# Earlier weight sums in the up projection, VectorE adds in the merges, and a first weight cast in two pieces: a two-layer hybrid decoder on one core

## The chip, the core and the metric

The kernel runs on one core of a Trainium2 chip. The core has five engines that work side by side, each with an instruction queue of its own: TensorE (in the profile PE, with its weight loads as PEld), VectorE (DVE), ScalarE (ACT), GpSimd (POOL) and SyncE (SP), which here only issues DMAs. GpSimd and ScalarE issue DMAs too. An engine takes its instructions in order; when the first one waits on a semaphore, what is behind it waits too. Matrix products are accumulated in PSUM, and everything else lives in SBUF.

The metric is the device time of one execution in microseconds (us), and the time of a kernel is the median over several executions.

## The reference

`reference()` is a trunk of `DEPTH` = 2 layers over `SEQ` = 512 tokens of width `D_MODEL` = 1024, all in float32. Cut to what matters:

```python
for l in range(DEPTH):
    h = rmsnorm(x, norm1_g[l])
    p = h @ w_in[l]
    p_rw, p_ret, p_sg, gate_logits = jnp.split(p, in_cuts, axis=-1)
    branches = jnp.stack([y_rw, y_ret, y_sg], axis=2)   # three token mixers
    proj = jnp.einsum('bsgc,gcd->bsgd', branches, w_branch[l])
    gates = jax.nn.sigmoid(gate_logits.reshape(B, S, N_BRANCH, D_MODEL))
    x = x + jnp.sum(gates * proj, axis=2) @ w_out[l]
    x = x + conv_ffn(rmsnorm(x, norm2_g[l]), ffn_w_up[l], ffn_conv_w[l], ffn_conv_b[l], ffn_w_down[l])
return rmsnorm(x, final_g)
```

`conv_ffn` multiplies by `ffn_w_up` (1024 x 5632), applies a causal convolution of width 3 along the tokens, multiplies silu(gate) by the value half, and multiplies by `ffn_w_down` (2816 x 1024).

## The kernel before

**Precision.** TensorE's fast format keeps only part of a float32 number. So each factor is split into a high part (a cast, by ScalarE) and a low part (the number less its high part, by VectorE), and each product is three matmuls: high by low, high by high, low by high (`mm3`, L190; the matmuls are booked under L194). A weight is read in units of 128x512: a load from HBM (`load`, L124, issued by SP into a tile `wr`), a cast (`part`, L175, tiles `wh` or `sh`) and a subtraction (L178, tiles `wl` or `sl`). A unit feeds twelve matmuls. The first pass over the program only notes the units in order; in the second pass this list is the plan by which loads and casts run some units ahead of the products (`unit`, L97; `AHEAD`, L32). The first unit of the plan has `npart` 0.

**The order of work.** The Tile framework orders the instructions of every engine with its own model of their times. `keep_in_program_order` and `kept` (L119) pin the instructions that they are given to the order of the program. In the feed-forward part the loads, casts and subtractions of the weights are kept so, and the weight sums below with them. Tiles come from pools: `acc` has four PSUM buffers, `f`, `u` and `r` hold SBUF tiles of 128x512.

**The start.** `firstK` (L369) multiplies the first units by the first blocks of x. The first weight, the first blocks of x and their norm factors are loaded in turns; a string of steps (L438) gives the order of casts (`w`) and norm products (`z`). A block's high part is made by VectorE for the first block and by ScalarE (L260) for the others, its low part by VectorE (L261). The first unit's matmuls are those of L383, the later ones those of L194.

**The merges.** For each of three branches and eight row blocks, `merge` (L1144) loads a stored gate (`gth<-gd`, L1148, a DMA on GpSimd's queue), multiplies one unit of branch weights by the branch's output into an `acc` tile, and multiplies gate and product on VectorE (L1151). Branch 0 starts the sum `mg[m]`; branch 2 and branch 1 add to it (L1154). For branch 2 (`br` 2, the digit 2 in `SEQ`, L30) GpSimd adds, and for branch 1 VectorE, since only that call passes `add` (L531). After branch 1 the sum is split into its parts (`split`, L182) for the output projection `wout` (L1157).

**The up projection.** `ffn_up` (L1174) computes 44 columns of 128 rows each, a gate column and a value column in turns, numbered `c` from 0. A column takes two units, 24 matmuls. VectorE takes it out of PSUM (L1202, tile `fu`), ScalarE and VectorE do the convolution (L1204 to L1206, tile `cv`), and after each second column come silu and the product (L1213, L1214). Every four columns the results are combined and split for the down projection (`halves`, L1224).

**The weight sums.** The down projection is a Strassen-like scheme that needs sums of blocks of `ffn_w_down`. A set is four raw 128x512 tiles of one block of that weight; from it four sums are made in place. In the up projection `presum` (L283) is called after every column: by the table `PRE` (L27), a set with start `at` has one raw tile loaded (L289, on SP's queue) in each of the columns `at` to `at`+3, and one sum made (L162, on VectorE) and stored to HBM (L304, on GpSimd's queue) in each of the columns `at`+4 to `at`+7. Layer 0 has nine sets, starting every four columns from 4 to 36, so that there is exactly one sum in each of the columns 8 to 43. Layer 1 has six, from 4 to 36, with gaps. The other sets are made elsewhere. The down projection (`down`, L1265, in layer 0; `last`, L1418, in layer 1) reads the sums back as weight units.

Of the kernel before, what the change touches and what calls it, by code (L numbers as in the profile page):

```python
# [13 lines left out]
ADD, SUB, MUL, POW, MAX = ALU.add, ALU.subtract, ALU.mult, ALU.pow, ALU.max  # L14
# [9 lines left out]
FIRST = (12, 4, 0, 8)  # L24
FILL = (36, 2, 1)
KEPT = 6
PRE = {0: {4 + 4 * k: 2 + k for k in range(9)}, 1: {4: 0, 10: 1, 16: 2, 22: 3, 29: 4, 36: 6}}  # L27
RSUM = {(0, 3): (0, 0), (0, 10): (0, 1), (1, 3): (1, 8), (1, 10): (1, 10)}
NOW = ((1, 5), (1, 7), (1, 9))
SEQ = "0 H G G 0 S 0 U U G G 0 S 0 0 S 2 2 Y 0 0 2 1 2 1 2 1 2 1 2 1 2 1 1 1"  # L30
# [23 lines left out]
class Emit:  # L54
# [109 lines left out]
    def part(self, u):  # L164
        raw, n, pool = self.raws.pop(0), u[4], u[5]
        if type(raw) is tuple:
            raw = self.sumnow(raw)

        self.turn = (self.turn + 1) % 5 if pool in ("p", "q") else 4
        if pool is None or self.turn < 3:  # L170
            hi, lo = [self.wp.tile([128, 512], F32R, name=self.nm(t), tag=t, bufs=3) for t in ("wh", "wl")]
        else:
            hi, lo = [{"f": self.f, "r": self.r, "u": self.u, "p": self.u, "q": self.u}[pool](dt=F32R, n=t) for t in ("sh", "sl")]
        with self.tc.high_priority() if pool in (None, "p", "q") else nullcontext():
            self.kept(self.nc.scalar.copy(hi[:, :n], raw[:, :n]))  # L175
            if self.raws and type(self.raws[0]) is tuple:
                self.sumnow(self.raws[0])
            self.kept(self.nc.vector.tensor_tensor(lo[:, :n], raw[:, :n], hi[:, :n], op=SUB))  # L178
        self.parts.append((hi, lo))
        self.npart += 1  # L180
# [102 lines left out]
    def presum(self, l, c):  # L283

        for at, q in PRE[l].items():
            n = c - at
            if 0 <= n < 4:
                self.pre[l, q, n] = t = (self.f if at < 21 else self.u if l or at in (28, 36) else self.r)(n="pre")
                self.kept(self.nc.sync.dma_start(t, self.raw4(l, q, (1, 3, 0, 2)[n])))  # L289
            if 4 <= n < 8:  # L290
                b = [self.pre[l, q, k] for k in (2, 0, 3, 1)]
                p = (7, 5, 6, 4)[n - 4]
                t, i = self.sum4(b, p)
                self.kept(i)
                self.stores.append(((l, q), p, t))
                self.store4(n=1)
# [188 lines left out]
    def mixer(self, l, nst):  # L485
        self.pool = None
        with self.tc.tile_pool(name=f"rw{l}", bufs=1) as rp:
            self.rwp = rp
            self.filler = self.fillers(l)
            st = self.rwkv(l, nst)  # L490
        for _ in self.filler:
            pass
        self.rp = self.tc.tile_pool(name=f"ff{l}", bufs=NFP)
        self.fp = self.rp.__enter__()
        self.gup, self.bs, self.ws = self.f(n="gup"), self.f((128, 4, 128), n="bs"), self.f((128, 4, 128), n="ws")
        with self.tc.high_priority():
            self.nc.sync.dma_start(self.gup, self.a["gup"][l])
        self.nc.sync.dma_start(self.bs.rearrange("p g i -> p (g i)"), self.a["sgb"][l:l + 1, :].to_broadcast([128, 512]))
        self.nc.sync.dma_start(self.ws, self.a["sgw"][l])
        self.pool = "f"  # L500
        sg, out = self.sgu_v(l), self.rwkv_out(l, *st)
        self.nc.vector.tensor_tensor(self.ws, self.ws, self.c("le").unsqueeze(1).to_broadcast([128, 4, 128]), op=MUL)
        self.qk = []
        for c in range(NC):
            self.qk.append(self.f(n="qkT"))
            self.turned(self.qk[c], self.f(n="qkt"), self.ro[c], self.nc.gpsimd)
        self.wsp = self.split(self.ws.rearrange("p g i -> p (g i)"), self.f)
        for step in (sg, sg, out, sg, out, sg, None, out, sg, out, sg):
            next(step) if step else self.sgu_bias()
        yrw, ysg, mg, out, m2 = self.yrw, [], [], [], 0  # L510
        self.pool = "r"
        rest = self.sgu_u(l, range(2, 4))
        rows = iter([((), (0, 1), (0, 1, 2)), ((0, 1), (2, 3)), ((2, 3),)])
        for step in SEQ.split():
            if step == "S":
                self.ret_pair(*next(rows))
            elif step == "G":
                ysg.append(self.sgu_out(len(ysg)))
            elif step == "H":
                self.ret_heads()  # L520
            elif step == "U":
                next(rest), next(rest)
            elif step == "Y":
                yret = self.ret_out()
            elif step == "0":
                mg.append(self.merge(l, 0, len(mg), yrw))
            elif step == "2":
                mg[m2] = self.merge(l, 2, m2, ysg, mg[m2])
                m2 += 1
            else:  # L530
                out.append(self.split(self.merge(l, 1, len(out), yret, mg[len(out)], self.nc.vector), self.f))  # L531
        return out

    def fillers(self, l):
# [606 lines left out]
        return self.split(t2, self.f)  # L1141


    def merge(self, l, br, m, y, sum=None, add=None):  # L1144

        nc = self.nc
        t = self.f(n="gth")
        nc.gpsimd.dma_start(t, self.gd[br, m])  # L1148
        ps = self.acc()
        self.matF(ps, ("wall", l, 58 + br * 4 + m // 2, m % 2 * 512), y)  # L1150
        nc.vector.scalar_tensor_tensor(t, t, 1.0, ps, op0=ADD, op1=MUL)  # L1151
        if sum is None:
            return t
        (add or nc.gpsimd).tensor_tensor(sum, sum, t, op=ADD)  # L1154
        return sum

    def wout(self, l, mg, xd, st):  # L1157
# [566 lines left out]
```

## Time and profile before

| | us |
|---|---|
| median of 3 runs (1688.55, 1686.04, 1684.36) | 1686.04 |
| the profiled execution | 1686.46 |
| its span, from the first to the last instruction | 1684.7 |

| engine | busy us | share of the span |
|---|---|---|
| TensorE, matmuls | 1673.6 | 99% |
| TensorE, weight loads | 1392.5 | 83% |
| VectorE | 1292.1 | 77% |
| ScalarE | 820.3 | 49% |
| GpSimd | 301.4 | 18% |

The granted clock of TensorE is 1.000 over the whole span. In layer 0 the last merges run from about 417 to 465 us, the up projection from about 500 to 733 and the down projection from there; in layer 1 the last merges run from about 1256 to 1304, and the up projection ends at about 1572.

A row of the timeline gives the start, the duration, engine, line and operation, what is written from what is read, the shape and the count, and in brackets how long the engine was idle before it and which instruction ended that. Durations of neighbouring rows overlap a little, because an engine starts the next instruction while the last one still writes; the cost of one in a full queue is the distance of the starts. A row of the waits gives who waited for whom, the total, how many times, and the longest. Matmul ends are modelled and reach past the start of the next matmul.

### The profile page before, as it was taken

Reading aid. Unit: us, or ns where it says so; the run is one execution under the profiler, and the core shown is the slowest. Engines: PE = TensorE matmul, PEld = TensorE weight load, DVE = VectorE, ACT = ScalarE, POOL = GpSimd, SP = SyncE. Lnnn points to the kernel's source line nnn. Section 1 sums busy time; section 2 is a strip of 40 time slices with the busy share of each in tenths; the row PEclk is TensorE's granted clock in tenths of the full one; section 3 lists DMA queues with packets and bytes.
Section 4 is the critical chain, followed back from the end, with each engine's and each line's share of the span. In section 5 each row is a group of like instructions: output and inputs, shape, how many; then the busy total and the mean of one; then the engine's idle time right before and its main releaser. Section 6 shows DMA issues by size and latency. Waiting matters only on the chain.

```text
span 1684.7 us, 29297 instructions
## 1 busy us (share of the span) xinstructions
PE 1673.6 (99%) x10643; PEld 1392.5 (83%) x10643; DVE 1292.1 (77%) x2289; ACT 820.3 (49%) x1436; POOL 301.4 (18%) x450
## 2 busy tenths in 40 slices
PE   9999999999999999999999999999999999999998
PEld 7888877888888888889988887778888888888887
DVE  7887746578668888877868877565785688898897
ACT  6563433554254444456655634335542544444565
POOL 1121013312210111110111210233122012221100
PEclk9999999999999999999999999999999999999999
DMA  5236655533553666678733366655344436664775
GB/s 183 88 109 205 192 185 172 186 125 128 177 188 115 204 202 217 219 233 301 234 114 94 106 195 188 201 164 188 122 143 149 156 131 201 207 209 161 273 243 176
DMA packets 158592, 298.38 MB, mean 177 GB/s; under 512 B 21936, under 2 KB 32944, under 8 KB 158448
## 3 DMA queue, kind: packets, MB, share of 16 engines
q1 hardware_dynamic: 128864, 217.12, 40.2%
q0 software_dynamic: 21232, 64.25, 11.5%
q10 hardware_dynamic: 8352, 15.15, 2.5%
q8 instruction: 83, 1.36, 0.3%
q14 instruction: 61, 0.50, 0.1%
HBM read 236.40 MB, written 60.03 MB: 176 GB/s over the span
## 4 chain that ended last, share of the span: by engine, by line
PE 87%; DVE 5%; issue 3%; DMA 3%; ACT 1%; POOL 1%; SPq 1%; ACTq 0%; DVEq 0%; POOLq 0%
PE acc L194 75%; PE sm L194 5%; PE sm L769 2%; DMA wr<-wall 1%; PE sm L1025 1%; DVE sl L178 1%; PE sm L676 1%; DVE cv L1205 1%; DVE fu L1202 1%; SPq L726 1%; DVE cv L1206 1%; DMA tr<-vT 0%; DVE wl L178 0%; PE sm L1136 0%; ACT cv L1204 0%
## 5 line engine op out<-in xcount | busy, mean ns | idle before, releaser
L194 PE MATMUL acc<-lo,sh 128*128 128x512 f32 (+1 forms) x1144 | 443.0, 387 | 0.4 <-DVE gth L1151 0.4
L194 PE MATMUL acc<-hi,sh 128*128 128x512 f32 (+1 forms) x1144 | 441.8, 386 | 0.0
L194 PE MATMUL acc<-hi,sl 128*128 128x512 f32 (+1 forms) x1144 | 429.3, 386 | 0.5 <-DVE sl L178 0.5
L175 ACT CAST sh<-wr 128x512 fp32r<-128x512 f32 x352 | 212.2, 616 | 213.2 <-DMA wr<-wall 100.5
L175 ACT CAST wh<-wr 128x512 fp32r<-128x512 f32 x278 | 171.4, 620 | 270.8 <-PE acc L194 178.7
L178 DVE TENSOR_TENSOR wl<-wr,wh 128x512 fp32r<-128x512 f32 x278 | 196.2, 708 | 136.7 <-ACT wh L175 130.8
L178 DVE TENSOR_TENSOR sl<-wr,sh 128x512 fp32r<-128x512 f32 x352 | 239.9, 695 | 72.3 <-ACT sh L175 63.5
L194 PEld LDWEIGHTS acc<-lo,sh 128*128 128x128 f32 x1144 | 214.9, 188 | 45.1 <-issue 1.4
L194 PEld LDWEIGHTS acc<-hi,sl 128*128 128x128 f32 x1144 | 214.9, 188 | 44.1 <-DVE sl L178 0.9
L194 PEld LDWEIGHTS acc<-hi,sh 128*128 128x128 f32 x1144 | 214.9, 188 | 42.8
L194 PE MATMUL acc<-lo,wh 128*128 128x512 f32 (+1 forms) x636 | 245.1, 385 | 0.2 <-ACT wh L175 0.2
L194 PE MATMUL acc<-hi,wl 128*128 128x512 f32 (+1 forms) x636 | 243.3, 383 | 0.1
L194 PE MATMUL acc<-hi,wh 128*128 128x512 f32 (+1 forms) x636 | 242.5, 381 | 0.0
L1204 ACT ACTIVATE cv<-fu,pc 128x512 f32<-128x512 f32 x88 | 71.8, 816 | 175.1 <-DVE fu L1202 175.0
L194 PEld LDWEIGHTS acc<-hi,wl 128*128 128x128 f32 x636 | 119.6, 188 | 25.1 <-DVE wl L178 1.4
L194 PEld LDWEIGHTS acc<-lo,wh 128*128 128x128 f32 x636 | 119.6, 188 | 24.3 <-ACT wh L175 1.0
L194 PEld LDWEIGHTS acc<-hi,wh 128*128 128x128 f32 x636 | 119.7, 188 | 22.3 <-issue 0.2
L1205 DVE SCALAR_TENSOR_TENSOR cv<-fu,pc,cv 128x511 f32<-128x511 f32 x88 | 65.9, 748 | 30.2 <-ACT cv L1204 29.7
L194 PE MATMUL acc<-wl,hi 128*128 128x512 f32 x212 | 85.8, 405 | 0.0
L194 PE MATMUL acc<-wh,hi 128*128 128x512 f32 x212 | 82.5, 389 | 0.0
L194 PE MATMUL acc<-wh,lo 128*128 128x512 f32 x212 | 82.5, 389 | 0.0
L1202 DVE TENSOR_TENSOR fu<-acc,rsF 128x512 f32<-128x512 f32 x88 | 60.3, 685 | 14.2 <-PE acc L194 13.1
(423 smaller groups left out, 2605.4 us busy)
## 6 DMA issues: line engine op xcount, KB each, us to landing
wr<-wall SPq DMA_DIRECT2D x480, 256.0 KB, 3.0
wr<-ts SPq DMA_DIRECT2D x76, 256.0 KB, 4.4
wr<-wdt SPq DMA_DIRECT2D x66, 256.0 KB, 3.7
pre<-wdt SPq DMA_DIRECT2D x60, 256.0 KB, 3.6
ts<-pre POOLq DMA_DIRECT2D x60, 256.0 KB, 2.9
gd<-gth ACTq DMA_DIRECT2D x48, 256.0 KB, 2.6
gth<-gd POOLq DMA_DIRECT2D x48, 256.0 KB, 3.7
sp<-ab SPq DMA_DIRECT2D x22, 256.0 KB, 4.7
```

The source lines that it names most:

```text
L175: self.kept(self.nc.scalar.copy(hi[:, :n], raw[:, :n]))
L178: self.kept(self.nc.vector.tensor_tensor(lo[:, :n], raw[:, :n], hi[:, :n], op=SUB))
L194: i = self.nc.tensor.matmul(*x, **y, **kw)
L676: i = T.matmul(pK[hv[1 - h], j, :], bk[hv[h], c, 1, :], x[hv[h], c, :], start=True, stop=True)
L726: nc.sync.dma_start(o[r:r + 32, :].rearrange("d (e x) -> d e x", e=2), d[hv[h], j * n:j * n + n].rearrange("(e d) x -> d e x", d=32))
L769: po(T.matmul(o, l, r, start=start, stop=True, skip_group_check=True))
L1025: po(T.matmul(o, lhsT, rhs, start=start, stop=stop, skip_group_check=True))
L1202: V.tensor_tensor(u, ps, self.rsF, op=MUL)
L1204: A.activation(t, u, AF.Identity, scale=self.p("cw2", j), bias=self.p("cb", j))
L1205: V.scalar_tensor_tensor(t[:, 1:], u[:, :511], self.p("cw1", j), t[:, 1:], op0=MUL, op1=ADD)
L1206: V.scalar_tensor_tensor(t[:, 2:], u[:, :510], self.p("cw0", j), t[:, 2:], op0=MUL, op1=ADD)
```

## The change

It has three parts.

1. The weight sums. In layer 0 the nine sets start at columns 4, 8, 12, 15, 19, 23, 26, 30, 34 instead of every fourth column up to 36. The sums now lie in the columns 8 to 41, with two in column 19 and two in column 30; the raw loads lie in the columns 4 to 37, with two in column 15 and two in column 26. In layer 1 the last two of six sets start at 28 and 34 instead of 29 and 36, and the last sums are in the columns 38 to 41. The choice of the pool for each set follows the new numbers, so that each set keeps its pool. The number of loads, sums and stores stays the same.
2. The merges. `merge` loses the argument `add`, and every sum, that of branch 2 too, is made by VectorE.
3. The first unit. In the second pass, `part` casts the high part of the first unit in two instructions of 256 columns each; every other unit is cast as before.

```diff
-PRE = {0: {4 + 4 * k: 2 + k for k in range(9)}, 1: {4: 0, 10: 1, 16: 2, 22: 3, 29: 4, 36: 6}}
+PRE = {0: {c: 2 + k for k, c in enumerate((4, 8, 12, 15, 19, 23, 26, 30, 34))}, 1: {4: 0, 10: 1, 16: 2, 22: 3, 28: 4, 34: 6}}
...
         with self.tc.high_priority() if pool in (None, "p", "q") else nullcontext():
-            self.kept(self.nc.scalar.copy(hi[:, :n], raw[:, :n]))
+            for h in (slice(0, 256), slice(256, 512)) if self.npart == 0 and self.plan else (slice(0, n),):
+                self.kept(self.nc.scalar.copy(hi[:, h], raw[:, h]))
...
             if 0 <= n < 4:
-                self.pre[l, q, n] = t = (self.f if at < 21 else self.u if l or at in (28, 36) else self.r)(n="pre")
+                self.pre[l, q, n] = t = (self.f if at < 20 else self.u if l or at in (26, 34) else self.r)(n="pre")
...
-                out.append(self.split(self.merge(l, 1, len(out), yret, mg[len(out)], self.nc.vector), self.f))
+                out.append(self.split(self.merge(l, 1, len(out), yret, mg[len(out)]), self.f))
...
-    def merge(self, l, br, m, y, sum=None, add=None):
+    def merge(self, l, br, m, y, sum=None):
...
-        (add or nc.gpsimd).tensor_tensor(sum, sum, t, op=ADD)
+        nc.vector.tensor_tensor(sum, sum, t, op=ADD)
```

## The prediction, made before the changed kernel was run

> **What bounds the kernel now.** I read the page first, then the waits of TensorE, then the chain of waits for the pace of a matmul, then the timeline at each place the change touches.
>
> ```profile
> span 1684.7 us, 29297 instructions
> ...
> PE 1673.6 (99%) x10643; PEld 1392.5 (83%) x10643; DVE 1292.1 (77%) x2289; ACT 820.3 (49%) x1436; POOL 301.4 (18%) x450
> ```
>
> TensorE (PE) is busy for 99% of the span; no other engine comes above 77%. Work taken off VectorE (DVE) or GpSimd (POOL) is therefore worth only what TensorE waits for them. The list of those waits is short:
>
> ```profile
> PE acc L194 <- DVE sl L178: 1.6, 2, 1.0
> PE acc L423 <- DVE rst L420: 1.5, 1, 1.5
> PE sm L693 <- ACT Y L681: 0.5, 1, 0.5
> PE acc L194 <- DVE gth L1151: 0.4, 1, 0.4
> PE sm L769 <- DVE s L831: 0.4, 2, 0.2
> PE acc L194 <- DVE fu L1202: 0.3, 1, 0.3
> PE acc L194 <- ACT wh L175: 0.2, 1, 0.2
> PE acc L194 <- ACT sh L175: 0.2, 1, 0.2
> ```
>
> The rows (total, count, longest) sum to 5.1 us, 1.5 of it before any input is there. A row understates its loss, because a matmul's modelled end reaches past the next one's start. The true loss at a wait is the distance of two starts less the pace of an unhindered matmul, and two rows of the chain give that pace:
>
> ```profile
> 125.58 70.97 PE acc L194 x313
> ...
> 798.19 15.84 PE sm L194 x132
> ```
>
> 70.97/313 = 0.227 us for 512 columns and 15.84/132 = 0.120 us for 256 (layer 0's down projection). All gains below are such losses.
>
> **Part 1: the first weight in halves.** ScalarE casts the first weight in two 256-column halves instead of one piece. The start before:
>
> ```profile
> 4.43 0.62 ACT L175 CAST wh<-wr 128x512 fp32r<-128x512 f32 x1 [0.53 <-DMA wr<-wk]
> 5.10 1.19 PE L383 MATMUL acc<-hi,wh 128*128 128x512 f32 x4
> 6.42 0.72 ACT L260 ACTIVATE hi<-x,x0g 128x512 fp32r<-128x512 f32 x1 [1.37 <-DMA x<-xT]
> 7.03 1.07 PE L383 MATMUL acc<-hi,wl 128*128 128x512 f32 x4
> 7.18 0.75 DVE L261 SCALAR_TENSOR_TENSOR lo<-x,x0g,hi 128x512 fp32r<-128x512 f32 x1 [1.05 <-ACT hi L260]
> 8.08 0.47 PE L194 MATMUL acc<-lo,wh 128*128 128x512 f32 x1
> ```
>
> What half a cast costs is in the group of the up projection's 256-column casts (busy time, then mean ns of one):
>
> ```profile
> L1240 ACT CAST ah<-fth 128x256 fp32r<-128x256 f32 x22 | 8.9, 404 | 9.1 <-DVE fth L1214 9.0
> ```
>
> A half costs 0.404 us against 0.62, so the first matmul can start about 0.2 us before 5.10. But the second weight block starts at 8.08 because its x-low part (7.18 + 0.75 = 7.93) follows the x-high part, which waited 1.37 us for the load of x. TensorE issues its last four matmuls from 7.03 and would be free at 7.03 + 4 x 0.227 = 7.94; it already waits 0.14 there. Starting earlier only lengthens that wait: gain 0. If the matmul waited for both halves, the second would end at most 0.19 us later (2 x 0.404 - 0.62), of which 0.14 is covered: at most 0.05 lost. The added cast delays nothing on ScalarE either, since 1.37 idle us follow. I take 0; ends 0 and -0.05.
>
> **Part 2: the second-branch sums (`br` 2) move from GpSimd to VectorE.** This is 8 adds in each layer. Layer 0's late merges:
>
> ```profile
> 442.24 0.69 DVE L1151 SCALAR_TENSOR_TENSOR gth<-gth,acc 128x512 f32<-128x512 f32 x1 [0.92 <-DMA gth<-gd]
> 443.01 1.28 POOL L1154 TENSOR_TENSOR gth<-gth,gth 128x512 f32<-128x512 f32 x1 [3.43 <-DVE gth L1151]
> 443.41 1.44 DVE L178 TENSOR_TENSOR sl<-wr,sh 128x512 fp32r<-128x512 f32 x1 [0.48 <-PE acc L194]
> 444.25 1.08 POOL L1148 DMA_DIRECT2D gth<-gd  x2
> ...
> 448.59 0.69 DVE L1151 SCALAR_TENSOR_TENSOR gth<-gth,acc 128x512 f32<-128x512 f32 x1 [0.37 <-DMA gth<-gd]
> 448.59 0.39 PE L194 MATMUL acc<-hi,sl 128*128 128x512 f32 x1
> 449.42 0.47 PE L194 MATMUL acc<-lo,sh 128*128 128x512 f32 x1 [0.45 <-DVE gth L1151]
> ```
>
> And the busy time of each engine over most of the last merges (the stretch and its length, then PE, weight loads, DVE, ACT, POOL):
>
> ```profile
> 417.00:465.00 48.00, 47.55 (x211) 39.05 (x210) 31.65 (x44) 12.76 (x21) 13.94 (x18) 1.00 0.52 165
> ```
>
> The timeline is one chain. The gate loads (L1148) are issued from GpSimd's own queue, in order, behind the add (L1154). The add waits for VectorE's product (L1151), which had itself waited 0.92 us for its gate. So the next pair of loads leaves at 444.25, the product waits for it until 448.59, and TensorE, needing the PSUM buffer which that product frees, starts at 449.42 instead of 448.59 + 0.227. Loss: 0.60 us. It is the only one in the merges: the waits have L1151 once, and layer 1's merges are not among them.
>
> After the change GpSimd has only loads to issue here. At worst a load's buffer is one that the add frees: product and add back to back on VectorE at about 0.61 us each (the spacing of the rows in part 3) end near 442.24 + 1.22 = 443.46, so loads leave about 0.8 us earlier and 0.60 is recovered. At best they leave merges earlier, with the same 0.60. If the loads do not move, 0. I take 0.60 in layer 0 and 0 in layer 1.
>
> The price is 8 x 0.61 = 4.9 us of VectorE per layer. In the stretch of the last row, which holds six of the eight adds, VectorE is busy 31.65 of 48 us, so 16 us are free for 6 x 0.61 = 3.7. Behind an add in VectorE's queue stand the weight low parts (L178); they lose 0.61 at most, and part of it was paid already: the low part at 443.41 took 1.44 us beside the GpSimd add, twice the 0.69 of the products around it. The Trainium skill, SBUF — State Buffer, "Who interferes with whom", says that a VectorE instruction with two SBUF inputs contends with a GpSimd one that reads SBUF, and whoever starts first blocks the other. The 1.44 agrees. By that rule the move gives back up to 1.44 - 0.69 = 0.75 us at each collision for 0.61 paid, and the sum is the same. Against the move speaks the Trainium skill, Perfetto Trace Analysis, "Optimizing Scalar/DVE Operations": if VectorE is saturated, work handed to ScalarE or even GpSimd may help. By that page the adds would cost up to 4.9 us per layer; with 31.65 of 48 us busy the trace does not show the saturation it asks for.
>
> **Part 3: the weight sums end two columns earlier.** Counting `c` from 0, a set starting at `at` is summed at `at`+4 to `at`+7. Layer 0's last set moves from 36 to 34, layer 1's too: sums in columns 38 to 41, none in 42 and 43. Layer 0's end before:
>
> ```profile
> 738.37 0.60 ACT L175 CAST sh<-wr 128x512 fp32r<-128x512 f32 x1
> ...
> 738.51 0.28 PE L194 MATMUL acc<-ah,sl 128*128 128x256 f32 x1
> 739.03 0.50 PE L194 MATMUL acc<-ah,sh 128*128 128x256 f32 x2 [0.24 <-ACT sh L175]
> 739.24 0.69 DVE L162 TENSOR_TENSOR pre<-pre,pre 128x512 f32<-128x512 f32 x1
> 739.84 0.68 DVE L178 TENSOR_TENSOR sl<-wr,sh 128x512 fp32r<-128x512 f32 x1
> 740.58 0.39 PE L194 MATMUL acc<-ah,sl 128*128 128x256 f32 x1 [1.04 <-DVE sl L178]
> ```
>
> TensorE loses 739.03 - 738.51 - 0.12 = 0.40 us for the cast and 740.58 - 739.03 - 0.24 = 1.31 us for the low part. The sum at 739.24 stands straight ahead of that low part; without it the low part starts 0.60 earlier (the cast ended at 738.97, so it doesn't hold it). I take 0.60. What is late next is the rest, 1.11 us: the cast, which stands behind others on ScalarE. Ends: 0, if the planner puts other work into the gap, and 1.71, if the freed time lets it pull the cast forward too. Layer 1's end:
>
> ```profile
> 1572.54 0.69 DVE L162 TENSOR_TENSOR pre<-pre,pre 128x512 f32<-128x512 f32 x1
> ...
> 1574.13 0.61 PE L194 MATMUL acc<-wh,ah 128*128 128x512 f32 x2
> ...
> 1574.35 0.69 DVE L1202 TENSOR_TENSOR fu<-acc,rsF 128x512 f32<-128x512 f32 x1
> ...
> 1575.09 0.50 PE L194 MATMUL acc<-wl,ah 128*128 128x512 f32 x1 [0.34 <-DVE fu L1202]
> ```
>
> TensorE waits for the last column's eviction (L1202): 1575.09 - 1574.13 - 2 x 0.227 = 0.51 us. The sum at 1572.54 is ahead of that eviction in VectorE's queue; without it the eviction comes about 0.60 earlier and the whole 0.51 goes. Ends 0 and 0.51.
>
> The moved sums crowd elsewhere. In layer 0 the nine sets now start at 4, 8, 12, 15, 19, 23, 26, 30, 34, so columns 19 and 30 hold two sums, and 15 and 26 two loads on SP's queue; each sum's store follows on GpSimd's. VectorE's next pauses, from the timeline, and the loads from the page's list of DMA issues (last number: us to landing):
>
> ```profile
> 619.29 0.69 DVE L1202 TENSOR_TENSOR fu<-acc,rsF 128x512 f32<-128x512 f32 x1 [1.16 <-PE acc L194]
> ...
> 684.57 0.69 DVE L1202 TENSOR_TENSOR fu<-acc,rsF 128x512 f32<-128x512 f32 x1 [0.89 <-PE acc L194]
> ```
>
> ```profile
> pre<-wdt SPq DMA_DIRECT2D x60, 256.0 KB, 3.6
> ```
>
> A column is 24 matmuls, 24 x 0.227 = 5.44 us, so these are the evictions of columns 22 and 34 (12 x 5.44 = 65.3 apart). VectorE stood idle 1.16 and 0.89 us before them, waiting for TensorE: what a second sum (0.61) in column 19 or 30 pushes back is made up there. In between TensorE is not held, since it needs an eviction's PSUM buffer (one of four) only columns later and the low parts are made units ahead. A load has four columns, 21.8 us, to land in 3.6; a second one delays the weight load queued behind it on SP by less than those 3.6. I take 0 for all of it, and at the other end 1.31 us (the largest wait above) at each of the two doubled sums. Layer 1's last two sets start at 28 and 34 and have no doubled column.
>
> **Sum.** 0.60 + 0.60 + 0.51 = 1.71 us. The profiled execution took 1686.46 us for a span of 1684.7, so it would become 1684.75; its time is 0.42 above the median of 1686.04, and from the median the forecast is 1686.04 - 1.71 = **1684.3 us**, 0.10%. A measurement tells about 0.3% (5.1 us) from no change, so this counts as no change.
>
> **The rivals.**
> First, **the waits are only handed on**: the cast keeps TensorE at layer 0's end, another queue entry takes the sums' places, the gate loads stay where they are. For it: 1.11 of the 1.71 us lost at layer 0's end stays anyway. Against: the three freed waits each have the removed instruction right ahead of them. 0 to 0.6 gained: 1685.8.
> Second, **more comes free**: layer 0's end loses all its 1.71 us, so 0.60 + 1.71 + 0.51 = 2.82: 1683.2. For it: ScalarE's share is 49%. Against: its cast keeps its place unless the order changes.
> Third, **slower**: VectorE's queue is overfull where two sums meet, in layer 0's columns 19 and 30. It decides once VectorE has no idle 0.61 us left before a low part is needed; the price is up to 1.31 at each, 2.62 together, so 1686.04 - 1.71 + 2.62 = 1686.95. For it: the planner orders each column anew, and VectorE does 77% of the span. Against: the two pauses above.
> That **the change doesn't do what it says** holds for part 1: halves that gain nothing, already 0 in the sum.
>
> **How the numbers follow.** Forecast 0.45, handed on 0.25, more 0.13, slower 0.17. The three times of before spread from 1684.36 to 1688.55, so each case carries about 2 us to either side. The range is 1681.3 (1683.2 - 1.9) to 1688.3 (1686.95 + 1.35). All cases lie within 0.3% (1680.98 to 1691.10); only an order far from before's, which no row prices, leaves it: faster 0.03, within 0.3% 0.92, slower 0.05.
>
> **What would show it.** Right: no wait of a matmul for L1151 or for L1202; the gate loads leave without an add ahead of them; at layer 0's end a wait for the low part of about 0.7 instead of 1.31; the first matmul near 4.9 but the second block still at 8.1. Wrong: a new matmul wait for low parts near 605 to 625 or 660 to 675 us, gate loads still paced by the merges, or a time outside the range, which only a reordering in a stage that the change doesn't touch could make.

## The result and the profile after

The changed kernel takes a median of 1690.57 us (17 runs, 1688.12 to 1695.11) against 1687.17 us for the kernel before (17 runs on the same chip, 1684.36 to 1690.42). The ratio is 1.0020 with a 95% interval of 1.0012 to 1.0028. The change costs 2.0 to 4.7 us where the prediction expected a gain of 1.71; the time lies 2.3 us above the range. A line of the timeline that is left out is marked by `...`.

The page of the changed kernel begins with the span and the engines' busy times:

```profile
span 1689.0 us, 29291 instructions
...
PE 1675.0 (99%) x10643; PEld 1393.0 (82%) x10643; DVE 1291.9 (76%) x2305; ACT 819.8 (49%) x1437; POOL 280.0 (17%) x434
```

VectorE has 16 instructions more and GpSimd 16 fewer, as the diff says, and yet VectorE's busy time is the same (1292.1 before). Part of the reason is in the groups of instructions, VectorE's adds of the merges before and then after (count, busy time, mean ns of one):

```profile
L1154 DVE TENSOR_TENSOR gth<-gth,gth 128x512 f32<-128x512 f32 x16 | 13.3, 832 | 1.1
```

```profile
L1155 DVE TENSOR_TENSOR gth<-gth,gth 128x512 f32<-128x512 f32 x32 | 21.5, 687 | 0.4
```

Twice as many adds cost 8.2 us more, not 13.3: a mean add took 832 ns while GpSimd made half of them, and 687 now that it makes none. Another part is in VectorE's `vt` operations, which stood beside two of GpSimd's adds in each layer, before and then after:

```profile
L1076 DVE SCALAR_TENSOR_TENSOR vt<-ry,rrr,vt 128x128 f32<-128x128 f32 x32 | 13.0, 472 | 0.0
```

```profile
L1077 DVE SCALAR_TENSOR_TENSOR vt<-ry,rrr,vt 128x128 f32<-128x128 f32 x32 | 8.7, 346 | 0.0
```

So in amount, the move is nearly free. TensorE's waits, in the same form as in the prediction, show where it is not:

```profile
PE acc L195 <- DVE gth L1152: 3.2, 2, 1.9
PE acc L424 <- DVE rst L421: 1.5, 1, 1.5
PE acc L195 <- ACT wh L176: 1.4, 2, 0.9
PE acc L195 <- ACT sh L176: 0.6, 2, 0.3
PE acc L195 <- DVE sl L179: 0.4, 1, 0.4
```

(These lines are one higher than before: L1152 is the product, L179 the weight low part, L1155 the add, L1149 the gate load.) The wait for the last column has gone, and of the two for low parts one is left, at 0.4. The 0.9 in the row of casts (`wh`) is at 1006.69 us, in a stretch to which the experiments come back. New are two waits for a product of a merge, 3.2 us together, one in each layer; the single one of before (0.4) has gone. The timeline of layer 0's place, in order of time:

```profile
439.02 1.22 POOL L1149 DMA_DIRECT2D gth<-gd  x2 [4.85 <-PE acc L195]
...
441.25 0.62 ACT L176 CAST sh<-wr 128x512 fp32r<-128x512 f32 x1 [0.97 <-PE acc L195]
...
441.69 0.69 DVE L188 TENSOR_TENSOR lo<-gth,hi 128x512 fp32r<-128x512 f32 x1
...
443.54 0.39 PE L195 MATMUL acc<-hi,sl 128*128 128x512 f32 x1
443.80 0.69 DVE L179 TENSOR_TENSOR sl<-wr,sh 128x512 fp32r<-128x512 f32 x1 [1.43 <-issue]
444.41 1.28 DVE L1152 SCALAR_TENSOR_TENSOR gth<-gth,acc 128x512 f32<-128x512 f32 x2
445.24 0.47 PE L195 MATMUL acc<-lo,sh 128*128 128x512 f32 x1 [1.30 <-DVE gth L1152]
```

The gate loads left at 439.02 with no add ahead of them, as predicted. But VectorE's rows show what happens next: it is idle for 1.43 us, then a weight low part, and only then the product for which TensorE stands still. In the kernel before, the product of this merge stood ahead of that low part (442.24, then 443.41, in the prediction's rows). The low part cannot start earlier: its cast ended at 441.87, yet it starts at 443.80, just when TensorE's last matmul has read its weight part (443.54 + 0.227 = 443.77). So, by these times, it waited for a buffer that this matmul freed. The pair's gates weren't late: in this trace the last gate of the layer landed at 442.93, while VectorE stood idle. TensorE waits for the product, the product stands behind the low part, and the low part waits for TensorE to use up all it has: the loss is 445.24 - 443.77 = 1.47 us up to the start of that matmul.

Layer 1's place, in the same view:

```profile
1285.38 0.39 PE L195 MATMUL acc<-hi,sl 128*128 128x512 f32 x1
1285.62 0.62 ACT L176 CAST sh<-wr 128x512 fp32r<-128x512 f32 x1 [1.58 <-issue]
1286.27 0.69 DVE L179 TENSOR_TENSOR sl<-wr,sh 128x512 fp32r<-128x512 f32 x1 [1.42 <-ACT sh L176]
1286.88 1.28 DVE L1152 SCALAR_TENSOR_TENSOR gth<-gth,acc 128x512 f32<-128x512 f32 x2
1287.70 0.47 PE L195 MATMUL acc<-lo,sh 128*128 128x512 f32 x1 [1.94 <-DVE gth L1152]
```

Here even the cast waits until TensorE's last matmul is through (1285.38 + 0.227 = 1285.61), so cast, low part and product come one after another: 1287.70 - 1285.61 = 2.09 us. The last gate of this layer landed at 1285.07. The kernel before has the two in the other order there, the pair of products first:

```profile
1281.36 1.35 DVE L1151 SCALAR_TENSOR_TENSOR gth<-gth,acc 128x512 f32<-128x512 f32 x2
1283.29 0.69 DVE L178 TENSOR_TENSOR sl<-wr,sh 128x512 fp32r<-128x512 f32 x1 [0.58 <-ACT sh L175]
```

The theory to test is thus **the order**: with the adds on VectorE, the framework sets products behind low parts that wait for TensorE. The rivals: VectorE's **added work** itself, the **earlier sums**, the **halves**, and **chance**, since one execution was compared with another.

### The profile page after: what moved, and what is told of

Its sections match the earlier page's. It is cut to its first block, busy times and chain, and to the rows that moved or that the text cites. A ratio compares the mean times of both kernels' runs of the same rounds, so it can differ in the third digit from the quotient of the medians.

```text
span 1689.0 us, 29291 instructions
## 1 busy us (share of the span) xinstructions
PE 1675.0 (99%) x10643; PEld 1393.0 (82%) x10643; DVE 1291.9 (76%) x2305; ACT 819.8 (49%) x1437; POOL 280.0 (17%) x434
## 4 chain that ended last, share of the span: by engine, by line
PE 93%; DVE 2%; DMA 2%; issue 1%; ACT 1%; POOL 0%; SPq 0%; ACTq 0%; DVEq 0%; POOLq 0%
PE acc L195 82%; PE sm L195 5%; PE sm L770 2%; PE sm L1026 1%; PE sm L677 1%; DMA wr<-wall 1%; DMA gd<-gth 0%; DMA tr<-bkT 0%; PE sm L1137 0%; DVE wl L179 0%; DMA bkS<-tr 0%; PE acc L424 0%; DVE cv L1207 0%; ACT wh L176 0%; DVE sl L179 0%
## 5 line engine op out<-in xcount | busy, mean ns | idle before, releaser
L176 ACT CAST wh<-wr 128x512 fp32r<-128x512 f32 (+1 forms) x279 | 171.3, 618 | 277.1 <-PE acc L195 179.2
L179 DVE TENSOR_TENSOR wl<-wr,wh 128x512 fp32r<-128x512 f32 x278 | 194.6, 703 | 143.1 <-ACT wh L176 137.3
L179 DVE TENSOR_TENSOR sl<-wr,sh 128x512 fp32r<-128x512 f32 x352 | 237.9, 690 | 68.5 <-ACT sh L176 58.8
L1203 DVE TENSOR_TENSOR fu<-acc,rsF 128x512 f32<-128x512 f32 x88 | 60.3, 685 | 13.3 <-PE acc L195 12.4
```

Of the source, the lines that this page charges most:

```text
L176: self.kept(self.nc.scalar.copy(hi[:, h], raw[:, h]))
L1203: V.tensor_tensor(u, ps, self.rsF, op=MUL)
```

## The experiments

All kernels are the kernel before with the edit shown; none leaves out a part of the computation. Timed ones ran 10 or 11 times, beside 21 to 32 runs of the kernel before on the same chip.

**One part at a time.** The sums alone (new table `PRE`, with the choice of pool that goes with it):

```diff
-PRE = {0: {4 + 4 * k: 2 + k for k in range(9)}, 1: {4: 0, 10: 1, 16: 2, 22: 3, 29: 4, 36: 6}}
+PRE = {0: {c: 2 + k for k, c in enumerate((4, 8, 12, 15, 19, 23, 26, 30, 34))}, 1: {4: 0, 10: 1, 16: 2, 22: 3, 28: 4, 34: 6}}
```

> Only the earlier weight sums (the second table and the pools that go with it); adds on GpSimd and the first cast whole, as before. If the loss of the whole change comes from the merges (theory of the order), this part alone is faster by about 1.5 us: the wait for a product of the up projection at 740 us (0.64) and those at 1575 and 1578 us (0.87) go, and no TensorE wait changes near 443 or 1285 us. If the sums are to blame (rival), it is slower by 1 us or more, with new waits at the doubled columns, 605 to 625 and 660 to 675 us. If the 2 us at 1004 to 1016 us of the changed kernel come from the change and not from one profile's transfers, they are either here or in the next run.

Measured: 1686.12 us, before 1686.42; ratio 0.9997 (0.9989 to 1.0006). Not slower: the sums are not to blame. The interval holds no gain, the 1.1 us of the prediction and the 1.5 expected here. The matmul starts, further below, show 0.9.

The adds alone:

```diff
-        (add or nc.gpsimd).tensor_tensor(sum, sum, t, op=ADD)
+        nc.vector.tensor_tensor(sum, sum, t, op=ADD)
```

> Only the eight adds of the second branch in each layer on VectorE; the old sums, the first cast whole. Theory of the order: TensorE waits about 1.4 us near 443 us and about 2 us near 1285 us for the product of a merge that now stands behind a weight low part, and gains 0.57 near 449 us, so slower by 2.5 to 3 us. Rival, that the two waits come from something else (the sums, transfers of one execution): within 0.6 us of before.

Measured: 1690.71 us; ratio 1.0023 (1.0014 to 1.0033), by it 3.9 us slower (2.4 to 5.6) and as slow as the whole change. That is more than the 2.5 to 3 expected: the 0.57 that was to be gained near 449 us did not come, as is explained below. Its TensorE waits:

```profile
PE acc L194 <- DVE gth L1151: 3.2, 2, 1.9
```

The loss is in this part. Whether order or work makes it is still open.

**The same work in another order.** One of the eight adds in each layer is put back on GpSimd. Which one decides the order that the framework makes:

```diff
-        (add or nc.gpsimd).tensor_tensor(sum, sum, t, op=ADD)
+        (add or (nc.vector if m != 5 else nc.gpsimd)).tensor_tensor(sum, sum, t, op=ADD)
```

> As the last, but the sixth of the eight adds (m of 5) stays on GpSimd; the other seven are on VectorE. With that one back, the framework sets the product ahead of the weight low part at both places, as in the kernel before, while seven eighths of VectorE's added work stay. Theory of the order: no TensorE wait for a product near 443 or 1285 us, the time from 0.6 us faster than before to 0.6 slower. Rival, VectorE's added work itself: seven eighths of the loss of the run with all eight, so 2.2 to 2.6 us slower.

> Seven adds on VectorE as in the run with the sixth left out, but here the first of the eight (m of 0) is the one that stays on GpSimd. The framework then sets the product behind the weight low part in layer 0 (as in the changed kernel) and ahead of it in layer 1. Theory of the order: a TensorE wait of about 1.3 us near 445 us and none near 1286 us, so about 1.4 us slower than the run with the sixth left out, near 1687.5 us. Rival, the amount of VectorE's work: the same time as that run, 1686.1 us, with no wait or with both.

> Again seven adds on VectorE; the last of the eight (m of 7) stays on GpSimd. The product stands behind the weight low part in both layers, as in the changed kernel. Theory of the order: TensorE waits of about 1.3 us near 445 us and 1.9 us near 1286 us, and a time near that of all eight adds, 3 to 4 us slower than before. Rival, the amount of VectorE's work: as the other two runs with seven adds, no more than 1 us from before.

(The two others have `m != 0` and `m != 7` in that line.)

| seven adds on VectorE, left on GpSimd | median us | before | ratio (95%) | longest wait for a product, layer 0 | layer 1 |
|---|---|---|---|---|---|
| the sixth (m of 5) | 1686.13 | 1686.42 | 1.0001 (0.9992 to 1.0010) | none | 0.28 |
| the first (m of 0) | 1689.35 | 1685.93 | 1.0024 (1.0015 to 1.0033) | 1.30 | 0.32 |
| the last (m of 7) | 1690.70 | 1685.93 | 1.0024 (1.0015 to 1.0033) | 1.30 | 1.94 |

Same number of adds, and the waits follow the order. Layer 0 with the sixth left out, VectorE's rows:

```profile
442.67 0.69 DVE L1151 SCALAR_TENSOR_TENSOR gth<-gth,acc 128x512 f32<-128x512 f32 x1 [0.95 <-DMA gth<-gd]
443.80 0.69 DVE L178 TENSOR_TENSOR sl<-wr,sh 128x512 fp32r<-128x512 f32 x1 [0.44 <-PE acc L194]
444.41 0.68 DVE L1154 TENSOR_TENSOR gth<-gth,gth 128x512 f32<-128x512 f32 x1
```

The low part waits here too, to the same 443.80, and here the profile names TensorE (PE) as what it waited for; but the product has already been made, and TensorE doesn't stop. With the first left out, the same place and the matmul behind it:

```profile
444.06 0.69 DVE L178 TENSOR_TENSOR sl<-wr,sh 128x512 fp32r<-128x512 f32 x1 [1.43 <-issue]
444.67 1.28 DVE L1151 SCALAR_TENSOR_TENSOR gth<-gth,acc 128x512 f32<-128x512 f32 x2
445.49 0.47 PE L194 MATMUL acc<-lo,sh 128*128 128x512 f32 x1 [1.30 <-DVE gth L1151]
```

Layer 1 shows a middle case, which was not expected. With the sixth or the first left out, one of the pair's two products is ahead of the low part and the other behind it. TensorE then waits 0.32 at this place (first left out) or 0.28 for a product about 5 us later (sixth left out), in place of 1.94. VectorE's rows with the sixth left out:

```profile
1282.52 0.68 DVE L1151 SCALAR_TENSOR_TENSOR gth<-gth,acc 128x512 f32<-128x512 f32 x1
1284.05 0.69 DVE L178 TENSOR_TENSOR sl<-wr,sh 128x512 fp32r<-128x512 f32 x1 [0.84 <-ACT sh L175]
...
1285.26 0.68 DVE L1151 SCALAR_TENSOR_TENSOR gth<-gth,acc 128x512 f32<-128x512 f32 x1
```

So the amount of VectorE's work falls as a cause, and the order stands. One number missed: the run with the first left out should have been 1.4 us above that with the sixth left out. It is 3.2 us above it by the medians, and 3.9 by the two ratios (the two ran on different chips). The matmul starts in the two merges account for 1.6 of that; the rest is not explained beyond the intervals, which are 1.5 us to either side for each run.

**The halves, and the change without its adds.**

```diff
-            self.kept(self.nc.scalar.copy(hi[:, :n], raw[:, :n]))
+            for h in (slice(0, 256), slice(256, 512)) if self.npart == 0 and self.plan else (slice(0, n),):
+                self.kept(self.nc.scalar.copy(hi[:, h], raw[:, h]))
```

> Only the first weight's high part cast in halves. The prediction's step: no difference (the second block of the first weight waits for x either way), within 0.3 us. Rival, that the two casts cost the start: the first matmuls near 5.6 in place of 4.9 us, still 0.5 us late at 8 us, which the later stages take up by 70 us, so again within 0.3 us in all but visible at the start; slower by 0.9 us if nothing takes it up.

Measured: 1687.44 us, before 1686.42; ratio 1.0007 (0.9998 to 1.0016). No difference that can be told (0.3 us faster to 2.7 slower), which is too wide to settle the 0.3 us expected. The start of this kernel, and after it that of the run with the adds alone, whose first cast is whole:

```profile
1.52 4.62 PE L423 MATMUL acc<-rst 128*128 128x256 f32 x10 [1.52 <-DVE rst L420]
5.60 1.46 PE L383 MATMUL acc<-hi,wh 128*128 128x512 f32 x4
```

```profile
1.52 4.63 PE L423 MATMUL acc<-rst 128*128 128x256 f32 x10 [1.52 <-DVE rst L420]
5.59 1.65 PE L383 MATMUL acc<-hi,wh 128*128 128x512 f32 x4
```

With halves or without, the first matmul comes at 5.6 as soon as ten warm-up matmuls on an empty tile are through. The 5.6 is neither a gain nor a loss of the halves.

> The change without its VectorE adds: earlier sums and the first cast in halves, all of branch 2's adds on GpSimd. Theory of the order: the whole loss is gone, 0 to 1.5 us faster than before (0.9 from the sums, 0 from the halves). Rival, that sums or halves take a part of the loss: slower than before by 1 us or more.

Measured: 1685.10 us, before 1685.93; ratio 0.9997 (0.9988 to 1.0005). Without the adds the loss is gone.

**What one execution does by itself.** Three more profiled executions, the first of the kernel with the sixth add left on GpSimd (its label speaks of sums, but the sums are those of before), then of both kernels of the comparison:

> The run with the sixth add left on GpSimd once more, for one look. Theory of the order: again no TensorE wait above 0.5 us for a product of a merge. Of the stages the edit does not touch (the start, 160 to 180, 891 and 1004 to 1068 us) the waits of its first look that come from transfers of one execution are gone or elsewhere.

> The kernel before, profiled once more. If the wait of 0.45 us for a product near 449 us, which the prediction took as a fixed term, was one slow transfer of one execution, it is not here, or of another length, and the TensorE shifts at the start and at 1004 to 1016 us differ too. If it is fixed, it is 0.4 to 0.5 us again, with GpSimd's gate loads at 444 us.

> The whole change, profiled once more. Theory of the order: the two waits for a product again, 1.3 us near 445 and 1.9 us near 1287 us, for they follow from the order and not from one execution; the 2 us at 1004 to 1016 us of its first profile, if a matter of transfers, are smaller or gone.

The first (1685.37 us) again has no wait for a product above 0.3 us. The kernel before, profiled again, has a span of 1682.1 us and no TensorE wait for a product at all. GpSimd's add and loads at the place that the prediction priced:

```profile
442.21 1.28 POOL L1154 TENSOR_TENSOR gth<-gth,gth 128x512 f32<-128x512 f32 x1 [3.11 <-DVE gth L1151]
443.44 1.09 POOL L1148 DMA_DIRECT2D gth<-gd  x2
```

and the product that needs them, without a wait for the load:

```profile
447.33 0.68 DVE L1151 SCALAR_TENSOR_TENSOR gth<-gth,acc 128x512 f32<-128x512 f32 x1
```

The loads still leave late, behind the add, and it doesn't matter: 3.89 us from their issue to the product here, 4.34 in the first profile. The transfer of the first of the two took 3.12 us here and 4.31 there. The 0.60 us was one execution's. In the second profile of the changed kernel the two waits are back:

```profile
444.57 0.47 PE L194 MATMUL acc<-lo,sh 128*128 128x512 f32 x1 [1.30 <-DVE gth L1151]
...
1283.60 0.47 PE L194 MATMUL acc<-lo,sh 128*128 128x512 f32 x1 [1.94 <-DVE gth L1151]
```

The same can be done for the whole program. TensorE runs 10643 matmuls in every kernel. The start of each is set against the start of the one with the same number in the second profile of the kernel before; the table gives by how much it falls behind (negative: gains) within a stretch of that profile, in us:

| kernel | 0 to 400 | 440 to 446 | 446 to 455 | 730 to 750 | 985 to 1240 | 1279 to 1287 | 1287 to 1450 | 1560 to 1585 |
|---|---|---|---|---|---|---|---|---|
| before, first profile | 0.49 | 0.00 | **0.70** | -0.01 | 1.17 | 0.00 | 0.13 | 0.25 |
| changed, first profile | 0.90 | **1.58** | -0.02 | **-0.59** | 3.33 | **2.19** | 0.07 | **-0.64** |
| changed, second profile | 0.23 | **1.57** | -0.03 | **-0.59** | 0.18 | **2.21** | 0.00 | **-0.62** |
| sums alone | 1.77 | 0.00 | 0.23 | **-0.33** | 2.44 | 0.00 | 0.43 | **-0.59** |
| adds alone | 0.90 | **1.57** | -0.03 | -0.01 | 1.57 | **2.18** | 0.00 | 0.13 |
| halves alone | 1.08 | 0.00 | -0.03 | 0.29 | 0.50 | 0.00 | 0.14 | 0.16 |
| adds but the sixth, first profile | 0.90 | 0.00 | 0.02 | -0.01 | 1.58 | 0.69 | 0.42 | 0.03 |
| adds but the sixth, second profile | 0.01 | 0.00 | 0.05 | -0.01 | 0.62 | 0.67 | -0.07 | 0.09 |
| adds but the first | 1.14 | **1.56** | -0.02 | 0.28 | 0.79 | 0.68 | 0.35 | 0.33 |
| adds but the last | 0.95 | **1.57** | -0.02 | 0.01 | 2.83 | **2.19** | -0.01 | 0.10 |
| sums and halves | 2.55 | 0.00 | 0.01 | **-0.59** | 1.69 | 0.00 | 0.01 | **-0.62** |

Four columns belong to the edits, and the profiles give them alike to about 0.3 us: the two merges and the two ends of the up projections. In the merges the numbers are 0.1 above the losses worked out from the rows, because the matmul after the late one comes late too. The column 446 to 455 holds the prediction's 0.60: of the five profiles with all of branch 2's adds on GpSimd, one has 0.70, one 0.23 and three nothing. The first and the fifth belong to the execution: 0 to 400 varies from 0 to 2.6 us and 985 to 1240 from 0 to 3.3, with the same kernel too (0.18 and 3.33 in the fifth for the changed one, where the wait at 1006.69 lies). The changed kernel's second profile is the one least disturbed there: 1.57 + 2.21 - 0.59 - 0.62 = 2.57 us slower, within the timed 2.0 to 4.7.

**Versions that might beat both.** The whole change, and the sums and adds without the halves, each with the sixth add left on GpSimd:

> The whole change, but the sixth of branch 2's adds (m of 5) stays on GpSimd in each layer. Theory of the order: the product stands ahead of the weight low part again at both places, so the waits of 1.3 and 1.9 us for a product are gone, and the time is 3 to 4.5 us below that of the whole change: 0.3 slower to 1.5 faster than before. Rival, that sums, halves and adds hurt only together: still 2 us or more slower than before.

> The earlier sums and the adds but the sixth on VectorE; the first cast whole. Theory of the order: as the run before, within 0.5 us of it, since the halves are worth nothing. Rival, that the halves cost a part of the start: faster than the run before by 0.5 to 1 us.

Measured: 1686.66 us and 1686.07 us, before 1686.12; ratios 0.9998 (0.9990 to 1.0007) and 0.9994 (0.9985 to 1.0003). One add put back in each layer takes away the loss of 3.4 us as far as the intervals tell. By the matmul starts, both still lose 0.7 us in layer 1's merges, and gain 1.2 and 0.9 at the two ends of the up projections. Neither version is shown to be faster than before, and the two can't be told apart.

## Why the prediction was wrong, step by step

**What bounds the kernel: right.** TensorE is 99% busy after as before, and all that changed is what it waits for.

**Part 1, the halves: right in the price, in part by luck, and wrong in a mark.** 0 was forecast, and no difference that can be told was measured. But the first matmul did not come near 4.9 nor the second block at 8.1; in the changed kernel's first profile they came at 5.59 and 8.98. The first matmul stands behind the warm-up matmuls, and these took 4.63 us in place of 3.85. Even in the first profile of the kernel before, the last of them starts at 4.99, so that 4.9 was out of reach. And the changed kernel's second block follows straight on the first (the four matmuls from 8.08, 8.08 + 4 x 0.227 = 8.99), without the wait for x on which the prediction's 0 rests. So the 0 came out in part for another reason than the one given.

**Part 2, the adds: this is the step that failed, twice.** The gain of 0.60 us was one execution's. The chain was read rightly, and the loads did leave earlier (the layer's last pair at 439.02 in place of 450.59). But whether a load that leaves behind an add comes too late depended on the transfer, and in the second profile of the kernel before it came in time. The price failed in the sentence "Behind an add in VectorE's queue stand the weight low parts (L178); they lose 0.61 at most". It takes the queue of before with adds put in, and the sum put the price at nothing. The framework orders the engine anew, and what moved was not a low part behind an add but a product behind a low part, which has no bound of 0.61: it costs the time until TensorE has freed the low part's buffer, and cast, low part and product after that, 1.47 and 2.09 us. That the adds give back on VectorE about what they cost there was right, and didn't matter. The free 16 us of VectorE were there, and no help: VectorE was idle while it held TensorE up.

The prediction did name "an order far from before's, which no row prices" and gave slower 0.05. It looked for it "in a stage that the change doesn't touch"; it came in the one that it touches. Its slower rival, the overfull queue in the doubled columns of the sums, did not come: between 455 and 730 us the changed kernel falls behind by 0.00.

**Part 3, the sums: right.** Layer 0's end gained 0.59 where 0.60 was forecast, and the rest stays as it was said to; TensorE's rows in the first profile of the changed kernel, then in the sums alone:

```profile
740.28 0.50 PE L195 MATMUL acc<-ah,sh 128*128 128x256 f32 x2 [0.24 <-ACT sh L176]
741.23 0.39 PE L195 MATMUL acc<-ah,sl 128*128 128x256 f32 x1 [0.44 <-DVE sl L179]
```

```profile
740.12 0.50 PE L194 MATMUL acc<-ah,sh 128*128 128x256 f32 x2 [0.52 <-ACT sh L175]
741.07 0.38 PE L194 MATMUL acc<-ah,sl 128*128 128x256 f32 x1 [0.45 <-DVE sl L178]
```

741.23 - 740.28 - 0.24 = 0.71, and the cast's wait is unchanged. The sums alone gain as much at the low part; their column shows 0.33, since the cast cost 0.28 more in that execution, as it did with the halves alone. Layer 1's end gained 0.59 to 0.64 against the second profile of before and 0.25 more against the first; 0.51 was forecast. The forecast had one wait there, the eviction, and missed another: in the second profile of before 0.40 us are lost at the eviction and 0.18 at a low part 3.6 us later, which also stands right behind a sum. With the sums moved both have gone. The timed runs with the sums cannot show a gain of this size.

**The sum.** Of 1.71 us forecast, about 1.2 came (part 3, where 1.11 was forecast), and the 0.60 was not there in most executions; 3.8 us were lost that were priced at nothing. Of the 6.3 us between forecast and measurement 1.1 belongs to neither: the forecast started from a median of 3 runs, 1686.04, and the median of 17 is 1687.17.

One thing stays open. In layer 1's up projection the changed kernel loses 0.7 us between 1365 and 1380 and gains 1.0 between 1430 and 1450, in both profiles: a wait for a cast is new at 1378.63 (0.35), and the wait for a low part at 1440.03 (0.52) has gone. The runs with the sixth add left out show the same (one of them gains only 0.6), the one with the first left out in part (0.7 and 0.45), those with all adds or all but the last on VectorE and the old sums not at all. So the order changed there too, where neither the adds nor the sums were edited. It cancels within 0.4 us, and no run was made for it. That the low parts waited for a buffer is read from the times of the rows, and from the one profile that names TensorE; a run with one buffer more was not made.

## What to carry to other kernels

Moving an instruction to an idle engine also hands the scheduler a new problem there, and the order it finds can cost more than the instruction: price a move by asking, for each wait of the bottleneck engine, what could come to stand ahead of the instruction that ends it, above all something that itself waits for the bottleneck. And a wait of half a microsecond behind a transfer is no term of a sum until a second execution has it too.

## What the runs showed of the hardware

The same ten warm-up matmuls do not take the same time in every execution. The first rows of TensorE in the kernel before, first profile, second profile, and in the changed kernel:

```profile
1.52 3.85 PE L423 MATMUL acc<-rst 128*128 128x256 f32 x10 [1.52 <-DVE rst L420]
```

```profile
1.52 4.14 PE L423 MATMUL acc<-rst 128*128 128x256 f32 x10 [1.52 <-DVE rst L420]
5.32 1.27 PE L383 MATMUL acc<-hi,wh 128*128 128x512 f32 x4
```

```profile
1.52 4.63 PE L424 MATMUL acc<-rst 128*128 128x256 f32 x10 [1.52 <-DVE rst L421]
5.59 1.73 PE L384 MATMUL acc<-hi,wh 128*128 128x512 f32 x4
```

They took 3.85, 4.14 and 4.63 us, and the four matmuls behind them 1.19, 1.27 and 1.73, while the mean granted clock over the whole span was 0.999 to 1.000 in all. Taken singly, the warm-up matmuls start 0.427 us apart at first; in the first profile of before the last ones start 0.216 apart, and in the changed kernel all stay at 0.427. The Trainium skill, TensorE: Matmul & The Clock Gate, "What you observe", says that TensorE's first matmuls run at about half the pace and that the change to full pace comes some 4 us into steady activity, up to 500 ns earlier or later from run to run. The rows agree on the half pace. They do not agree on the spread: by the starts the change comes at about 4.5 us in the first profile of before, 5.0 in the second, 6.5 in the changed kernel's first and 7.6 in the run with the sums alone, which is 3.0 to 6.1 us behind the first warm-up matmul at 1.52. What was measured here is thus wider, and it decides: a start within a microsecond of another says nothing about a change there.

The stretch from 985 to 1240 us took up to 3.33 us longer than in the quickest profile, as much as the change itself costs. In the changed kernel's first profile nearly all of it lies between 1000 and 1020 us. Ahead of the cast that ends TensorE's wait of 0.92 us at 1006.69, ScalarE stood idle for 3.52 us, by the profile for a transfer; no run was made to find what varies there. Single profiles of one kernel differ by 2.6 us in span (1684.7 and 1682.1 for the kernel before) and by 4.0 (1689.0 and 1685.0 for the changed one).
